# Moving the split weights of a decoder layer's plain products to another place within 256 bytes of SBUF

## The chip, the core and the metric

The kernel runs on one core of a Trainium2 chip. The metric is the device time of one execution in microseconds; lower is better. Most executions of it agree within 0.3%. One further execution was profiled, and all rows shown here come from such profiles.

## What is computed

One layer of a decoder over 512 prompt positions and 64 sample positions (8 sequences of 8), 576 columns together, with D_MODEL = 1024 and D_FF = 2816:

```python
def decoder_layer(x, c, pos0, S0, w_ada, b_ada, ...):
    m = silu(c) @ w_ada + b_ada                  # nine shift/scale/gate vectors
    h = modulate(rms_norm(x, n1_g), sh1, sc1)
    x = x + 0.5 * g1 * swiglu(h, w1_gate, w1_up, w1_down)
    h = modulate(rms_norm(x, nm_g), sh2, sc2)
    mix, S_new, v_rows = token_mix(h, ..., w_in, ..., w_a, w_b, w_o)   # gMLP branch and retention branch, merged
    x = x + g2 * mix
    h = modulate(rms_norm(x, n2_g), sh3, sc3)
    x = x + 0.5 * g3 * swiglu(h, w2_gate, w2_up, w2_down)
    return x, S_new, v_rows

def swiglu(h, w_gate, w_up, w_down):
    return (silu(h @ w_gate) * (h @ w_up)) @ w_down
```

All arrays are float32.

## The kernel before

**Split operands.** The large products run in TensorE's fp32r form. To keep float32 accuracy, every operand is split into a high part (ScalarE casts it, line 187, 195, 669 or 952) and a low part (VectorE subtracts, line 188, 196, 679 or 957). A product of two split operands is three matmuls for each slice of 128 rows of the contraction: high by high, high by low, low by high. Each matmul loads its own 128 x 128 weights first; the weight load of the next matmul runs while the present one streams its moving operand.

**Two kinds of product.** The products with the gate, up and most w_in matrices use a scheme with seven products of half blocks (`prod`, line 651): the moving operand is 288 columns wide. Everything else that multiplies by split weights, the plain products, goes through `proj` (line 485): the down projections w1_down and w2_down (tiles `wd`, some in `whl` and `xw`), w_b, the u columns of w_in and w_a (tiles `whl`) and w_o (tiles `whl`, `xw`, `wd` and one `wo`). `proj` makes an output of 576 columns in two PSUM banks, 320 columns wide and 256 columns wide:

```python
        for k in ks or range(kc):
            xh, xl = X[k]
            for z, (s, m) in enumerate(((wh, xh), (wh, xl), (wl, xh))):
                PE.matmul(
                    ps[:, :PW[h]], lhsT=s[:, k, c0:c0 + P], rhs=m[:, PART[h]],
```

Here `lhsT` is the stationary operand, the weights, and `rhs` the moving one. The values products (lines 1353 and 1583) have the roles the other way round: the operand `xx` is stationary and the split weights `whl` move.

**Places in SBUF.** The tile of a pair of split weights is a few words longer than its content, and `set_in` puts the content some words behind the tile's start:

```python
        t = home.tile([P, n + room], F32R, **kw)[:, at:at + n]
```

`at` is INTO = 28 words (112 bytes) for the seven-product weights and for the weights of lines 1353 and 1583. It is MID for the plain products. What follows counts addresses within one partition, modulo 256 bytes; the rows of all tiles concerned keep that place from slice to slice except where noted. In the compiled program the moving operands of `proj` (tiles `c`, `xx`, `xa`) all begin at 128, and so do the tiles `wd`, `whl` and `xw`; with MID = 16 words their weights lie at 192, which is 64 bytes on from the moving operand. The one tile `wo` (output block 7 of w_o, in the pool `hb_pool`) begins at 0, so its weights lie at 64, which is 192 bytes on. In `prod` the rows of the operand are 1152 bytes, four and a half times 256, so the weights lie 112 and 240 bytes on in turn. In lines 1353 and 1583 the stationary operand lies 144 bytes on from the moving weights.

**Order.** The Tile framework orders instructions by data and by the order in which they are written; at the changes of stage an order written by hand (`BEGIN`, `INTO_MIX`, `INTO_FFN2`) is kept on each engine. Weights come from HBM on the SyncE queue into `wraw` tiles. Three or four tile buffers (`whl`) or two (`wd`) let splits run ahead of the products.

**Names.** `home_wd`, `home1`, `home_whl` and `home_o` choose the tile for one output block's down or w_o weights; `nine_w` is the `xw` home, `whl` the general one. `load_w(..., at=MID)` serves w_b, u and w_a.

Of the kernel before, what the change touches and what calls it, by code (L numbers as in the profile page):

```python
# [35 lines left out]
GROUPS = (5, 6, 5, 6)  # L36

INTO = 28
MID = 16
HALF = (slice(0, H), slice(H, T))  # L40
PART = (slice(0, 320), slice(320, T))
PW = (320, T - 320)
# [42 lines left out]
def layer_kernel(ctx: ExitStack, tc: tile.TileContext, a):  # L85
# [24 lines left out]
    def nm(s):  # L110
        count[0] += 1
        return f"{s}_{count[0]}"
# [5 lines left out]
    def pool(stack, name, side="left"):  # L118
        return stack.enter_context(tc.tile_pool(name=nm(name), bufs=1, side=side, reuse_waits="tile"))
# [17 lines left out]
    def nine_w(shape):  # L137

        room = 9 * 256 - shape[1] * shape[2] * shape[3]
        return set_in(now["xs1"], shape, room, MID, tag="x", name=nm("xw"), bufs=3)  # L140

# [6 lines left out]
    def set_in(home, shape, room=INTO, at=INTO, **kw):  # L148

        n = 1  # L150
        for d in shape[1:]:
            n *= d
        t = home.tile([P, n + room], F32R, **kw)[:, at:at + n]
        if len(shape) == 4:
            return t.rearrange("p (a b c) -> p a b c", b=shape[2], c=shape[3])
        return t.rearrange("p (a b c d) -> p a b c d", b=shape[2], c=shape[3], d=shape[4])
# [9 lines left out]
    def whl(shape, at=INTO):  # L166
        small = len(shape) == 3 and shape[1] == 1
        tag = "whs" if small else "whl"
        return set_in(
            now["whs"] if small else wp, [P] + shape, INTO if small else 64, at,  # L170
            tag=tag, name=nm(tag), bufs=1 if small else 4,
        )
# [18 lines left out]
    def load_w(src, k0, kc, c0, cols, eng=None, at=INTO):  # L191
        return split_w(load_raw(src, k0, kc, c0, cols), eng, at)
# [772 lines left out]
    def home_wd(c, shape):  # L965
        return set_in(now["hl"], shape, 64, MID, tag="wd", name=nm("wd"), bufs=2)

    def home_whl(c, shape):
        return home_wd(c, shape) if c in (0, 1, 4, 5) else whl(shape[1:], MID)

# [163 lines left out]
    def home1(c, shape):  # L1134
        if c in (6, 7):
            return nine_w(shape)
        return home_wd(c, shape) if c in (0, 1, 4, 5) else whl(shape[1:], MID)

# [400 lines left out]
    def weights_b(hds, j):  # L1539
        kc = 2 * len(hds)  # L1540
        return load_w(a["w_b"][0], 2 * hds[0], kc, j * (8 // kc) * P, 8 // kc * P, at=MID)

# [112 lines left out]
    def weights_u(g):  # L1655
        return load_w(win, 0, KC, U0 + g * P, P, at=MID)

# [154 lines left out]
    def home_o(c, shape):  # L1812
        if c < 2:
            return whl(shape[1:], MID)
        if c < 5:
            return nine_w(shape)
        return home_wd(c, shape) if c < 7 else set_in(hb_pool, shape, INTO, MID, tag="wo", name=nm("wo"), bufs=1)

    Wo = Down(a["w_o"][0], 0, KC, home_o)
    late = []  # L1820

# [48 lines left out]
    hb_pool = pool(greg, "hb", "right")  # L1870
# [184 lines left out]
```

## Time and profile before

| | us |
|---|---|
| median of 3 runs (lowest, highest) | 1661.5 (1661.2, 1664.42) |
| the profiled execution | 1662.69 |
| its span, first to last instruction | 1660.9 |
| TensorE matmuls busy (12548 of them) | 1628.6 (98% of the span) |
| VectorE busy | 1153.0 (69%) |
| ScalarE busy | 783.1 (47%) |
| GpSimd busy | 293.4 (18%) |

The mean granted TensorE clock is 0.996. Lines 651 and 485 hold the largest groups of matmuls. A matmul's duration in the rows is longer than the time from its start to the next one's start, because matmuls are pipelined: the duration of "one" holds the way through the array as well as the streaming. Where matmuls run back to back, a stretch of the timeline gives the step from start to start: its length, less one duration, over the count less one.

### The profile page before, as it was taken

To read this page: it belongs to the slowest core of one execution; us is meant where nothing else is said; L and a number is where in the kernel's file an instruction comes from. 1 tells how busy PE (TensorE), PEld (TensorE's weight loads), DVE (VectorE), ACT (ScalarE), POOL (GpSimd) and SP (SyncE) were. 2 spreads that over 40 slices of the span, in tenths; PEclk is the share of its full clock that TensorE was granted. 3 is DMA by queue.
4 is the path that set the end of the run, shared out by engine and by line. 5 is a ranking of instruction groups with operands and counts; after the bars stand their busy time and mean duration, and the time that the engine had idled before them with its cause. 6 is when DMAs were issued, how large, how long until landed. Compare 5 with 4: busy or idle time off the path is not lost. (4 is left out here: it accounts for less than half of the span.)

```text
span 1660.9 us, 31368 instructions
## 1 busy us (share of the span) xinstructions
PE 1628.6 (98%) x12548; PEld 1566.4 (94%) x12548; DVE 1153.0 (69%) x1835; ACT 783.1 (47%) x1331; POOL 293.4 (18%) x372
## 2 busy tenths in 40 slices
PE   7999999999999999999999999999999999999997
PEld 4899999999999999999999999998999999999997
DVE  6867857576697777854788554676748868576773
ACT  5634524344564556553444453453236535343454
POOL 0000000000411111113346343454231000000002
PEclk9999999999999999999999999999999999999999
DMA  9553444332536776765467574799540333332321
GB/s 300 144 157 107 140 135 132 114 104 87 178 118 208 225 217 190 220 192 184 128 195 243 175 176 153 218 257 268 165 140 13 87 93 97 94 90 82 98 88 58
DMA packets 300212, 252.09 MB, mean 152 GB/s; under 512 B 13593, under 2 KB 260633, under 8 KB 300066
## 3 DMA queue, kind: packets, MB, share of 16 engines
q1 hardware_dynamic: 284594, 206.76, 41.3%
q0 software_dynamic: 13168, 40.97, 8.9%
q10 hardware_dynamic: 2304, 2.36, 0.4%
q8 instruction: 98, 1.61, 0.4%
q14 instruction: 48, 0.39, 0.1%
HBM read 207.01 MB, written 43.02 MB: 151 GB/s over the span
## 5 line engine op out<-in xcount | busy, mean ns | idle before, releaser
L651 PE MATMUL ps<-xa,whl 128*128 128x288 f32 x3000 | 422.2, 295 | 6.0 <-ACT xa L564 2.6
L651 PEld LDWEIGHTS ps<-xa,whl 128*128 128x128 f32 x3000 | 403.1, 190 | 18.7 <-issue 5.0
L651 PE MATMUL ps<-xs,whl 128*128 128x288 f32 x2040 | 289.1, 295 | 0.8 <-ACT sn L660 0.6
L651 PEld LDWEIGHTS ps<-xs,whl 128*128 128x128 f32 x2040 | 274.0, 189 | 11.0 <-issue 5.0
L679 DVE TENSOR_TENSOR whl<-wraw,whl 128x1024 fp32r<-128x1024 f32 x192 | 234.3, 1222 | 54.6 <-ACT whl L669 46.4
L669 ACT CAST whl<-wraw 128x1024 fp32r<-128x1024 f32 x192 | 200.0, 1047 | 107.7 <-DVE wraw L793 67.0
L485 PEld LDWEIGHTS ps<-c,wd 128*128 128x128 f32 x1824 | 240.1, 188 | 3.5 <-issue 3.4
L485 PE MATMUL ps<-c,wd 128*128 128x320 f32 (+1 forms) x1824 | 243.3, 294 | 0.0
L485 PE MATMUL ps<-c,whl 128*128 128x256 f32 (+1 forms) x1368 | 189.6, 296 | 1.1 <-ACT c L195 0.7
L485 PEld LDWEIGHTS ps<-c,whl 128*128 128x128 f32 x1368 | 182.0, 188 | 3.3 <-ACT c L195 1.0
L472 POOL TENSOR_TENSOR x<-x,s 128x64 f32<-128x64 f32 x72 | 36.9, 513 | 801.0 <-DVE s L471 773.5
L466 DVE SCALAR_TENSOR_TENSOR x<-ps,gate,x 128x320 f32<-128x320 f32 (+1 forms) x128 | 61.1, 481 | 115.4 <-PE ps L485 115.4
L660 ACT COPY sn<-ps 128x288 f32<-128x288 f32 x195 | 77.2, 398 | 105.1 <-PE ps L651 104.9
L188 DVE TENSOR_TENSOR whl<-wraw,whl 128x1024 fp32r<-128x1024 f32 x56 | 76.6, 1370 | 66.0 <-ACT whl L187 63.4
L952 ACT CAST wd<-wraw 128x640 fp32r<-128x640 f32 (+2 forms) x58 | 45.3, 781 | 105.3 <-PE ps L485 96.0
L1353 PE MATMUL ps<-whl,xx 128*128 128x256 f32 x768 | 88.9, 276 | 0.0
L1353 PEld LDWEIGHTS ps<-whl,xx 128*128 128x128 f32 x768 | 88.1, 188 | 0.0
L651 PE MATMUL ps<-xs,whs 128*128 128x288 f32 x480 | 69.9, 294 | 0.0
L187 ACT CAST whl<-wraw 128x1024 fp32r<-128x1024 f32 x56 | 58.5, 1048 | 22.3 <-PE ps L485 14.2
L651 PEld LDWEIGHTS ps<-xs,whs 128*128 128x128 f32 x480 | 65.7, 189 | 0.0
L669 ACT CAST whs<-wraw 128x512 fp32r<-128x512 f32 x62 | 38.5, 620 | 56.0 <-PE ps L651 46.8
L957 DVE TENSOR_TENSOR wd<-wraw,wd 128x640 fp32r<-128x640 f32 (+2 forms) x58 | 53.3, 920 | 10.6 <-ACT wd L952 10.5
(285 smaller groups left out, 2219.4 us busy)
## 6 DMA issues: line engine op xcount, KB each, us to landing
ada<-in_w_ada_dram SPq DMA_DIRECT2D x56, 512.0 KB
wraw<-in_w_in_dram SPq DMA_DIRECT2D x96, 256.0 KB
wraw<-in_w_gate_dram SPq DMA_DIRECT2D x88, 256.0 KB
wraw<-in_w_up_dram SPq DMA_DIRECT2D x88, 256.0 KB
wraw<-in_w_in_dram SPq DMA_DIRECT2D x32, 512.0 KB
wraw<-in_w_down_dram SPq DMA_DIRECT2D x32, 384.0 KB
wraw<-in_w_down_dram SPq DMA_DIRECT2D x32, 320.0 KB
accd<-c POOLq DMA_DIRECT2D x32, 288.0 KB, 5.4
```

The source lines that it names most:

```text
L187: ACT.copy(out=hi, in_=raw)
L188: now["lo"] = (eng or DVE).tensor_tensor(out=lo, in0=raw, in1=hi.bitcast(F32), op=ALU.subtract)
L466: DVE.scalar_tensor_tensor(out=x[:, o:o + w], in0=ps[:, :w], scalar=g[:, c, 0:1], in1=x[:, o:o + w], op0=ALU.mult, op1=ALU.add)
L472: return lambda: POOL.tensor_tensor(out=x[:, NP:T], in0=x[:, NP:T], in1=u, op=ALU.add)
L485: PE.matmul(ps[:, :PW[h]], lhsT=s[:, k, c0:c0 + P], rhs=m[:, PART[h]], start=k == 0 and z == 0, stop=k == kc - 1 and z == 2,)
L651: PE.matmul(ps[:, :H], lhsT=s[:, j * P:(j + 1) * P], rhs=m[:, j, :], start=fresh and j == 0 and z == 0, stop=j == 3 and z == 2, skip_group ...
L660: ACT.copy(out=t, in_=ps[:, :H])
L669: ACT.copy(out=hl[:, 0], in_=src)
L679: now["lo"] = DVE.tensor_tensor(out=hl[:, 1], in0=src, in1=hl[:, 0].bitcast(F32), op=ALU.subtract)
L952: ACT.copy(out=hl[:, 0], in_=self.raw[c])
L957: DVE.tensor_tensor(out=lo, in0=self.raw[c], in1=hi.bitcast(F32), op=ALU.subtract)
L1353: PE.matmul(ps[:, :DV], lhsT=s, rhs=m, start=i == 0, stop=i == 23)
```

## The change

The constant MID becomes 45 words, and the tile `wo`, which has no room for it, keeps 16. Tile sizes stay as they are. In the places above: the weights of the plain products go from 192 to 52 (308 less 256), that is from 64 to 180 bytes on from the moving operand. `wo` stays 192 on, the seven-product weights and lines 1353 and 1583 stay as they were. All former places are multiples of 16 bytes; 180 is 11 times 16 and 4 more.

```diff
-MID = 16
+MID = 45
...
         if c < 2:
             return whl(shape[1:], MID)
         if c < 5:
             return nine_w(shape)
-        return home_wd(c, shape) if c < 7 else set_in(hb_pool, shape, INTO, MID, tag="wo", name=nm("wo"), bufs=1)
+        return home_wd(c, shape) if c < 7 else set_in(hb_pool, shape, INTO, 16, tag="wo", name=nm("wo"), bufs=1)
```

## The prediction

> **What bounds the kernel now.** I read the page's busy times first, then the chain of waits, then TensorE's own waits, then the groups of instructions by shape, and last single stretches of the timeline.
>
> ```profile
> PE 1628.6 (98%) x12548; PEld 1566.4 (94%) x12548; DVE 1153.0 (69%) x1835; ACT 783.1 (47%) x1331; POOL 293.4 (18%) x372
> ...
> PEclk9999999999999999999999999999999999999999
> ```
>
> TensorE is busy for 98% of the span at full clock. The longest wait of a matmul is 4.4 us, and line 485, the plain products, has two rows in that view, 1.1 us together:
>
> ```profile
> PE ps L302 <- ACT ada L299: 4.4, 1, 4.4
> ...
> PE ps L485 <- ACT c L195: 0.7, 1, 0.7
> ...
> PE ps L485 <- DVE c L196: 0.4, 1, 0.4
> ```
>
> So the time is the number of matmuls by the step from one start to the next, and a change of place in SBUF can matter only through that step. The step isn't one number. Two pieces of the chain of waits hold down products alone, eight output blocks of the second feed-forward part each, half of the matmuls 320 wide and half 256 wide; columns are start, length, line and count:
>
> ```profile
> 1325.37 31.21 PE ps L485 x240
> ...
> 1423.21 38.08 PE ps L485 x288
> ```
>
> 31.21/240 is 130.0 ns for a matmul, 38.08/288 is 132.2 ns, with the same place and the same code. By shape (count, busy us, mean ns of one), the first stage and then the second:
>
> ```profile
> L485 PE MATMUL ps<-c,wd 128*128 128x320 f32 x120 | 18.9, 308 | 0.0
> L485 PE MATMUL ps<-c,wd 128*128 128x256 f32 x120 | 14.9, 276 | 0.0
> ```
> ```profile
> L485 PE MATMUL ps<-c,wd 128*128 128x320 f32 x144 | 22.4, 308 | 0.0
> L485 PE MATMUL ps<-c,wd 128*128 128x256 f32 x143 | 18.1, 281 | 0.0
> ```
>
> The 320-wide matmul is the same in both; the 256-wide one takes 276 ns or 281 ns. It runs in one of two steps, and once in one it stays there for a stage. The 5 ns per 256-wide matmul are half of that per matmul of the mix, which is the 2.2 ns between 130.0 and 132.2.
>
> **The change, part by part.** No instruction, wait, transfer or tile size is added, taken away or moved to another queue. Three sorts of work touch the new place: the weight loads of line 485, the matmuls that stream while the next load reads, and the splits that write there.
>
> *The matmuls.* The trace shows three places at work. At 64 bytes on there are both steps, as above. The nearest rows to 180 lie on either side of it, 192 (tile `wo`) and 144 (line 1353):
>
> ```profile
> 1241.69 3.68 PE L485 MATMUL ps<-xa,wo 128*128 128x320 f32 x24
> ...
> 1253.86 2.88 PE L485 MATMUL ps<-xa,wo 128*128 128x256 f32 x24
> ```
> ```profile
> L485 PEld LDWEIGHTS ps<-xa,wo x48: 187/188/188, 1241.5 to 1256.4; 128*128 128x128 f32 x48
> L485 PE MATMUL ps<-xa,wo x48: 276/292/308, 1241.7 to 1256.5; 128*128 128x320 f32 x24, 128*128 128x256 f32 x24
> ```
> ```profile
> L1353 PE MATMUL ps<-whl,xx x768: 275/275/362, 741.8 to 1101.9; 128*128 128x256 f32 x192
> ```
>
> The first fence is the timeline (start, length, line, count), the others give the shortest, median and longest duration. At 192 the 256-wide step is (2.88 - 0.276)/23 = 113.2 ns, and the 320-wide one (3.68 - 0.308)/23 = 146.6 ns. At 144 the 256-wide matmul takes 275 ns at the median of 768. Both neighbours have the fast 256-wide step, and the one that shows the 320-wide matmul has it as it was. So I take: 256 wide always at 276, 320 wide unchanged at 308.
>
> What that is worth: the groups of the whole run that are 256 wide and move to the new place, with the largest of the 320-wide ones:
>
> ```profile
> L485 PE MATMUL ps<-c,wd 128*128 128x320 f32 x912 | 143.3, 309 | 0.0
> L485 PE MATMUL ps<-c,wd 128*128 128x256 f32 x912 | 115.2, 279 | 0.0
> ...
> L485 PE MATMUL ps<-c,whl 128*128 128x256 f32 x684 | 90.3, 281 | 0.0
> ...
> L485 PE MATMUL ps<-xx,whl 128*128 128x256 f32 x192 | 23.9, 281 | 0.0
> ...
> L485 PE MATMUL ps<-xa,xw 128*128 128x256 f32 x72 | 8.9, 279 | 0.0
> ```
>
> Above 276 these hold 912 x 3 + 684 x 5 + 192 x 5 + 72 x 3 = 7.3 us; the four small groups left over (132 matmuls, `xa,whl`, `xa,wd`, `c,xw`) add at most 0.7 us at 5 ns. That 8.0 us is a ceiling: the means hold matmuls that waited for their data, and those stay (the longest of `c,whl` is 498 ns, in the row below). If the rows were pure mixtures of 276 and 281, 60% of the first and fourth and all of the others would be slow, 1,600 of 1,992; with the waits taken off I put it at half, 1,000, and by 2.2 ns x 2 = 4.4 ns each that is **4.4 us**. The floor of this term is 0 (the slow step stays as frequent), and below nothing it is the 1,000 fast ones turning slow, +4.4 us.
>
> ```profile
> L485 PE MATMUL ps<-c,whl x1368: 276/304/498, 415.9 to 1650.0; 128*128 128x320 f32 x98, 128*128 128x256 f32 x98
> ```
>
> *The 320-wide matmuls.* At 64 and at 192 they take 308 ns. Bounds by one step of the trace, the 5 ns between 276 and 281, either way: 1,992 x 5 ns = 10.0 us less or more. I take 0, the value at the nearest place.
>
> *The weight loads.* A load of 128 columns takes 188 ns; the loads of the `wo` tile never more than that, those of other plain products at times 192 (next fence). They run beside the matmul before, so I cost the change in them at nothing; the matmul of 113 ns is the cover, and what it costs without cover is the rival "one line more" below.
>
> *The splits.* ScalarE's cast of a 1024-column pair takes 1047 ns at place 112 (line 669) and 1048 at place 64 (line 187, MID); VectorE's subtraction 1222 ns (line 679) and 1214 ns in `wo`. So these don't follow the place among multiples of 16 bytes. No row shows a write at another multiple of 4; the slowest group of that shape, line 188, bounds it at 1370 ns, 156 ns more.
>
> ```profile
> L485 PEld LDWEIGHTS ps<-c,wd x1824: 186/188/192, 110.4 to 1643.7; 128*128 128x128 f32 x183
> ```
> ```profile
> L679 DVE TENSOR_TENSOR whl<-wraw,whl 128x1024 fp32r<-128x1024 f32 x192 | 234.3, 1222 | 54.6 <-ACT whl L669 46.4 <-DMA wraw<-in_w_in_dram 1.9 <-DMA ada<-in_w_ada_dram 1.6
> L669 ACT CAST whl<-wraw 128x1024 fp32r<-128x1024 f32 x192 | 200.0, 1047 | 107.7 <-DVE wraw L793 67.0 <-PE ps L651 31.1 <-DMA wraw<-in_w_up_dram 6.3
> ...
> L188 DVE TENSOR_TENSOR whl<-wraw,whl 128x1024 fp32r<-128x1024 f32 x56 | 76.6, 1370 | 66.0 <-ACT whl L187 63.4 <-DMA c<-in_gm_wsT_dram 1.8
> L187 ACT CAST whl<-wraw 128x1024 fp32r<-128x1024 f32 x56 | 58.5, 1048 | 22.3 <-PE ps L485 14.2 <-PE ps L1366 3.8 <-PE ps L1583 2.8
> ```
> ```profile
> L957 DVE TENSOR_TENSOR wo<-wraw,wo x1: 1214/1214/1214, 1225.4 to 1225.4; 128x1024 fp32r<-128x1024 f32 x1
> ```
>
> Some 100 pairs are written there (71 of the down and w_o products, 32 of w_b, u and w_a), so the bound is 16 us of VectorE's time over the whole run. VectorE is idle for 31% of the span and the plain products hardly wait for it, so I take nothing; if it did reach TensorE, the matmuls after a change of stage would show it first, waiting for `wd` or `whl`.
>
> *The sum.* 4.4 us off the profiled execution's 1662.69 gives 1658.3; that execution lies 1.2 us over the median of 1661.5, and its span 1.8 us under its own time. Against the median: 1661.5 - 4.4 = **1657.1 us**.
>
> **The rivals.**
>
> *No change.* Which of the two steps a stage falls into may follow from how the stage before left the pipeline and not from the place. For it: at 64 both appear with the same code. Against it: 768 matmuls at 144 have the fast one at the median. It gives 1661.5. The Trainium skill would have this one, or even less: "TensorE: Matmul & The Clock Gate", Part 2, says that the streaming operand and the weight load have two independent read ports of SBUF, so that loading the next weights takes no read bandwidth from the running matmul. By that rule no place matters and the sum is 0. The next row, of one line and one width, spreads from 289 to 298 ns within a group that hardly waits, and what alternates in it is the place (112 and 240 bytes on), so I give the rule less weight than the neighbours' rows.
>
> ```profile
> L651 PE MATMUL ps<-xs,whs x480: 289/294/298, 68.3 to 1598.7; 128*128 128x288 f32 x160
> ```
>
> *One line more (slower).* 180 is the only place that is no multiple of 16 bytes, so a row of 128 weights (512 bytes) lies in 33 pieces of 16 bytes and not in 32. What a piece costs: a load of 32 columns takes 108 ns and one of 128 takes 188, so 80/96 = 0.83 ns a column and 3.3 ns for four. A whole load of 128 columns reads for about 107 ns by that rate, 6 ns less than the fast step of 113. From the point where the extra piece, or a collision that it causes, is more than these 6 ns, the matmul waits. Paid by each of the 3,984 matmuls, 3.3 ns makes 13.1 us: 1674.6. The same size comes out if the 320-wide matmuls take a step of 5 ns (10.0 us) and the other 256-wide ones fall into the slow step (4.4 us): 1675.9.
>
> ```profile
> L307 PEld LDWEIGHTS ps<-ada,cs x224: 106/108/110, 79.4 to 737.2; 128*32 128x32 f32 x112
> ```
>
> The Trainium skill speaks for this one: "SBUF — State Buffer", section "Door 1: The DMA port swizzle", says that SBUF is read in lines of 16 bytes and that each access that crosses into a new line pays. No run here yet shows a weight load that begins within a line.
>
> *The 320-wide matmul gains a step too (faster).* If the odd place takes the load's reads out of the way of the stream altogether, the 320-wide matmuls fall by 5 ns as well: 1661.5 - 4.4 - 10.0 = 1647.1. For it: a 320-wide step of 146.6 ns is 33.4 ns longer than the fast 256-wide one for 64 columns more, 0.52 ns a column, where the 256-wide one pays 113.2/256 = 0.44, so there is time in it that the columns don't explain: at 0.44 ns it would be 141. Against it: it is 308 ns at both places that the trace has.
>
> **How the numbers follow.** The forecast (256 wide all fast, 320 wide as before) has 0.37. No change has 0.20, the slower rival 0.27 (nothing in the trace rules it out, and it is the only new kind of address), the faster one 0.16. A change of 0.2%, 3.3 us, is about what a measurement of this kernel can tell from none; the forecast's 4.4 us is little over it, so some of it (0.05) counts as no change. Faster: 0.32 + 0.16 = 0.48; same 0.25; slower 0.27. The forecast's own range is 1653.5 (the ceiling of 8.0 us) to 1660. The range to hold 8 in 10 reaches from 1644, a little below the faster rival, to 1675.5, over the slower one's 13.1 us.
>
> **What would show it.** In the changed kernel's rows of line 485 by shape, the 256-wide groups should read 276 to 278 where they read 279 to 281, and the 320-wide ones 308 to 309. The two pieces of the chain that were 31.21 us and 38.08 us should both come to 130.0 ns a matmul. The loads should stay at 188 ns. Lines 651, 1353 and 1583 should not move. The prediction is wrong if the 320-wide rows move at all, if weight loads read over 191 ns (one line more), or if the casts and subtractions into `wd` get longer and TensorE waits for them.

## The result, and the profile after

The changed kernel takes 1656.37 us at the median of six runs (1652.59 to 1658.16), the kernel before 1661.54 us at the median of six beside it (1661.11 to 1664.42). The ratio is 0.9962, with a 95% interval of 0.9948 to 0.9975. The forecast was 1657.1 us. The time came out as forecast; two of the steps that led to it did not.

The page of the changed kernel first. Its span was 1660.9 us before:

```profile
span 1654.4 us, 31368 instructions
...
PE 1624.5 (98%) x12548; PEld 1560.9 (94%) x12548; DVE 1153.0 (70%) x1835; ACT 784.3 (47%) x1331; POOL 293.1 (18%) x372
```

As many matmuls as before, TensorE as full as before, and a span 6.5 us shorter: the matmuls themselves follow each other faster. The chain of waits holds the two stages that the prediction showed, in the same order (start, length, line and count):

```profile
1320.89 30.95 PE ps L485 x240
...
1418.41 36.98 PE ps L485 x288
```

They were 31.21 and 38.08 us. That is now 129.0 ns and 128.4 ns a matmul; the forecast was 130.0 in both. The stage that already ran in the faster step lost time as well, which the forecast has no term for. The groups by shape show where from (count, then busy us and mean ns of one), the whole run first, then the first and the second of the two stages:

```profile
L485 PE MATMUL ps<-c,wd 128*128 128x320 f32 x912 | 140.6, 306 | 0.0
L485 PE MATMUL ps<-c,wd 128*128 128x256 f32 x912 | 114.6, 278 | 0.0
L485 PE MATMUL ps<-c,whl 128*128 128x320 f32 x684 | 111.0, 310 | 1.1 <-ACT c L195 0.7 <-DVE c L196 0.4
L485 PE MATMUL ps<-c,whl 128*128 128x256 f32 x684 | 89.2, 279 | 0.0
L485 PE MATMUL ps<-xx,whl 128*128 128x320 f32 x192 | 29.5, 309 | 0.0
L485 PE MATMUL ps<-xx,whl 128*128 128x256 f32 x192 | 24.0, 281 | 0.0
...
L485 PE MATMUL ps<-xa,wd 128*128 128x256 f32 x48 | 6.0, 285 | 0.0
```
```profile
L485 PE MATMUL ps<-c,wd 128*128 128x320 f32 x120 | 18.5, 306 | 0.0
L485 PE MATMUL ps<-c,wd 128*128 128x256 f32 x120 | 15.1, 277 | 0.0
```
```profile
L485 PE MATMUL ps<-c,wd 128*128 128x320 f32 x144 | 22.0, 306 | 0.0
L485 PE MATMUL ps<-c,wd 128*128 128x256 f32 x144 | 17.6, 276 | 0.0
```

In the first stage the 320-wide matmuls alone gain (18.9 us before); the 256-wide ones, all fast before, are 0.2 us slower. The rows of before that the prediction did not show:

```profile
L485 PE MATMUL ps<-c,whl 128*128 128x320 f32 x684 | 112.5, 312 | 1.1 <-ACT c L195 0.7 <-DVE c L196 0.4
...
L485 PE MATMUL ps<-xx,whl 128*128 128x320 f32 x192 | 30.0, 311 | 0.0
```

The three large groups of 320-wide matmuls went from 143.3 + 112.5 + 30.0 = 285.8 us to 281.1, those of 256-wide ones from 115.2 + 90.3 + 23.9 = 229.4 us to 227.8. With the small groups, line 485 loses 5.4 us in its 320-wide and 1.6 us in its 256-wide matmuls, 7.0 us together. The 6.5 us of the span are these 7.0 less small shifts in other lines and waits.

The rest stayed. These are the loads (shortest, median, longest), and the groups of the lines whose places did not change:

```profile
L485 PEld LDWEIGHTS ps<-c,wd x1824: 186/188/193, 110.3 to 1637.2; 128*128 128x128 f32 x183
```
```profile
L651 PE MATMUL ps<-xs,whl 128*128 128x288 f32 x2040 | 289.1, 295 | 0.9 <-ACT sn L660 0.5
...
L1353 PE MATMUL ps<-whl,xx 128*128 128x256 f32 x768 | 88.9, 276 | 0.0
...
L957 DVE TENSOR_TENSOR wd<-wraw,wd 128x640 fp32r<-128x640 f32 x32 | 27.5, 859 | 5.4 <-ACT wd L952 5.4
L952 ACT CAST wd<-wraw 128x640 fp32r<-128x640 f32 x32 | 23.3, 728 | 63.6 <-PE ps L485 56.1 <-DMA wraw<-in_w_down_dram 4.3 <-DMA wraw<-in_w_gate_dram 3.1
```

The last two, the split of a 640-column pair into `wd`, took 857 ns and 727 ns before.

Below, the *step* is the time from one matmul's start to the next one's, taken from the single records, with steps over 160 ns (waits) left out: some 1,970 steps of 320-wide and 1,983 of 256-wide matmuls. Over the whole run it went from 146.6 to 143.7 ns (320 wide) and from 115.5 to 114.8 ns (256 wide). By that count the change is 1,970 x 2.9 = 5.7 us and 1,983 x 0.7 = 1.4 us, the same picture as the busy times.

### The profile page after: what moved, and what is told of

Same layout as the page of the kernel before. It is cut to its first block, busy times and chain, and to the rows that moved or that the text cites. A ratio compares the mean times of both kernels' runs of the same rounds, so it can differ in the third digit from the quotient of the medians.

```text
span 1654.4 us, 31368 instructions
## 1 busy us (share of the span) xinstructions
PE 1624.5 (98%) x12548; PEld 1560.9 (94%) x12548; DVE 1153.0 (70%) x1835; ACT 784.3 (47%) x1331; POOL 293.1 (18%) x372
## 5 line engine op out<-in xcount | busy, mean ns | idle before, releaser
L651 PE MATMUL ps<-xs,whl 128*128 128x288 f32 x2040 | 289.1, 295 | 0.9 <-ACT sn L660 0.5
L1353 PE MATMUL ps<-whl,xx 128*128 128x256 f32 x768 | 88.9, 276 | 0.0
```

The costliest lines, as they stand in the source:

```text
L651: PE.matmul(ps[:, :H], lhsT=s[:, j * P:(j + 1) * P], rhs=m[:, j, :], start=fresh and j == 0 and z == 0, stop=j == 3 and z == 2, skip_group ...
L1353: PE.matmul(ps[:, :DV], lhsT=s, rhs=m, start=i == 0, stop=i == 23)
```

## The experiments

All edits are against the changed kernel; ratios are to the kernel before, measured beside each.

**Is it the word, the neighbourhood, or the multiple of 4?** After the result there were three readings. One: 180 itself is a good word. Two: any place off a multiple of 16 bytes is, since the reads of load and stream then no longer meet. Three: what decides is the broader neighbourhood, or what the stage before left in the pipeline, so that words near 180 give the same. Four kernels move MID alone; in the first, MID = 44 puts the weights 176 bytes on.

```diff
-MID = 45
+MID = 44
```

> One word less: weights 176 bytes on from the moving operand, on a multiple of 16 bytes. Theory 'place' (only how many bytes on the weights lie decides the step, and the start within a 16-byte line does not): as with 180, 320-wide steps alternate 142 and 145 ns (mean 143.5, duration 306), 256-wide mostly 113.3; about 1656 us, ratio to before 0.996 to 0.998. Rival 'line start' (180 is faster because a row of weights begins off a multiple of 16 bytes, so that the load's reads fall between the stream's): back to 146.7 ns (duration 308) for 320 wide and a mix of 113 and 118 for 256 wide; 1660 to 1662 us, ratio 0.999 to 1.0.

The same line with 17 (68 on, off a multiple of 16 by 4 bytes as 180 is, and on the same place within 16 bytes):

> One word more than before: weights 68 bytes on, off a multiple of 16 bytes by 4 as 180 is. 'Place': as at 64, 320-wide 146.7 ns (duration 308), 256-wide half at 113 and half at 118; 1661 us, ratio 0.999 to 1.001. 'Line start': as at 180, 320-wide 143.5 (306), 256-wide mostly 113; about 1656 us, ratio 0.996 to 0.998.

With 48 (192 on, the place of `wo`, one of the two rows on which the forecast rested):

> Weights 192 bytes on, the place of the tile wo of the kernel before, on which the forecast rested. If that tile's rows stand for the place: 256-wide always 113.3 ns (duration 276), 320-wide 146.6 (308); the gain comes from the 256-wide ones alone, about 4 us, 1657 us, ratio 0.997. If wo only carried on the step that the tiles before it had fallen into ('state'): 256-wide a mix of 113 and 118 as at 64, 320-wide 146.6; 1661 us, ratio 0.999 to 1.001.

With 29 (116 on, 64 bytes ahead of 180, so the same place within 64):

> Weights 116 bytes on: the same place within 64 bytes as 180 (52 past a multiple of 64), one block of 64 bytes earlier, and off a multiple of 16 by 4. If the place within 64 bytes decides: as at 180, 320-wide 143.5 ns (306), about 1656 us, ratio 0.996 to 0.998. If the place within 256 bytes does: nothing ties it to 180; 320-wide then 146.7 or another step (141 to 150), 1650 to 1672 us. 'Line start' alone gives the same as at 180.

All four are slower than the kernel *before*, which no reading of the first three had forecast: ratios 1.0033 (1.002 to 1.0045), 1.0036 (1.0023 to 1.0048), 1.0026 (1.0016 to 1.0035) and 1.0034 (1.0024 to 1.0045). By shape, 176 on and then 192 on:

```profile
L485 PE MATMUL ps<-c,wd 128*128 128x320 f32 x912 | 143.6, 309 | 0.0
L485 PE MATMUL ps<-c,wd 128*128 128x256 f32 x912 | 117.9, 281 | 0.0
```
```profile
L485 PE MATMUL ps<-c,wd 128*128 128x320 f32 x912 | 143.4, 309 | 0.0
L485 PE MATMUL ps<-c,wd 128*128 128x256 f32 x912 | 117.5, 280 | 0.0
```

The 320-wide matmuls are back at 309, and the 256-wide ones are slower than at 64. Four bytes off 180, the gain is gone. So neither the neighbourhood nor the place within 16 or 64 bytes explains it. And the forecast's own support falls: with all plain weights at 192, the place at which the 24 matmuls of `wo` had shown 113.2 ns, the mean step is 117.6 ns.

**The other neighbour, the period, and the weights of the other lines.** MID = 46 is 184 on, the neighbour above. MID = 36 is 144 on, the other row of the forecast (line 1353), now with load and stream in the plain products' roles:

> Weights 184 bytes on, one word past 180. Theory 'window' (good places form a stretch, and 176 lies just outside its lower end): 320-wide steps 143.5 ns or less (duration 306), 256-wide mostly 113; 1653 to 1658 us, ratio 0.995 to 0.998. Theory 'word' (the step is set word by word, and 180 is a single good word): 320-wide 146.7 (308), 256-wide near 118 (281 and over) as at 176 and 192; 1666 to 1670 us, ratio 1.002 to 1.005.

> Weights 144 bytes on, the distance that the values products of line 1353 have with the roles exchanged, and at which all their 256-wide matmuls run at 113.3 ns. If the distance alone sets the step, whichever of the two operands is the weights: 256-wide 113.3 ns (duration 275 to 276); with 320-wide at 146.7 that is 1657 us, ratio 0.997. If the roles matter, or those rows only carry on a fast step: 256-wide near 118 as at 176 and 192, 1666 to 1670 us, ratio 1.002 to 1.005.

184 on gives 1.0027 (1.0017 to 1.0038), 144 on 1.0043 (1.0029 to 1.0057). By shape, 184 and then 144:

```profile
L485 PE MATMUL ps<-c,wd 128*128 128x320 f32 x912 | 143.4, 308 | 0.0
L485 PE MATMUL ps<-c,wd 128*128 128x256 f32 x912 | 117.7, 281 | 0.0
```
```profile
L485 PE MATMUL ps<-c,wd 128*128 128x320 f32 x912 | 143.7, 310 | 0.0
L485 PE MATMUL ps<-c,wd 128*128 128x256 f32 x912 | 119.1, 284 | 0.0
```

180 stands alone between 176 and 184. At 144 the 256-wide matmul takes 284 ns, where line 1353's takes 275, though in both the stationary operand lies 144 bytes on from the moving one. So that row was no neighbour of this case, and distance and width alone don't set the step. What else differs: in line 1353 the weights are the moving operand, its operands begin at other places, and of its three matmuls the first two share the moving operand, where in `proj` they share the stationary one. Which of these counts was not run.

Next the tiles `wd` alone are moved on by 256 bytes more, to ask whether the place counts modulo 256:

```diff
-        return set_in(now["hl"], shape, 64, MID, tag="wd", name=nm("wd"), bufs=2)
+        return set_in(now["hl"], shape, 128, MID + 64, tag="wd", name=nm("wd"), bufs=2)
```

> As the changed kernel, but the weights in the tiles wd (about half of the plain products) begin 64 words further, at 256 + 180 bytes; the others stay at 180. If the place counts modulo 256 bytes: steps of the wd rows as at 180 (320-wide 143.5, 256-wide mostly 113), 1656 us, ratio to before 0.996 to 0.998. If it counts modulo more than 256: wd rows like those at 176 or 192 (146.7 and 118), half of the gain lost and as much added, 1660 to 1664 us.

The ratio is 0.9957 (0.9944 to 0.9969), the same as the change's within the intervals:

```profile
L485 PE MATMUL ps<-c,wd 128*128 128x320 f32 x912 | 140.6, 306 | 0.0
L485 PE MATMUL ps<-c,wd 128*128 128x256 f32 x912 | 114.6, 278 | 0.0
```

So 256 bytes more change nothing that the measurement can tell, where 4 do. Last in this group, INTO = 45 gives the seven-product weights and those of lines 1353 and 1583 the same words behind the tile's start:

```diff
-INTO = 28
+INTO = 45
...
-            now["whs"] if small else wp, [P] + shape, INTO if small else 64, at,
+            now["whs"] if small else wp, [P] + shape, 64, at,
...
-        return home_wd(c, shape) if c < 7 else set_in(hb_pool, shape, INTO, 16, tag="wo", name=nm("wo"), bufs=1)
+        return home_wd(c, shape) if c < 7 else set_in(hb_pool, shape, 28, 16, tag="wo", name=nm("wo"), bufs=1)
```

> As the changed kernel, and the seven-product weights too begin 45 words behind their tile's start: 180 and 52 bytes on in turn (112 and 240 before), the stationary operand of lines 1353 and 1583 76 bytes on from the moving weights (144 before). If 180 is a good word at any width: the 288-wide steps at 180 fall to 127 ns or less; with those at 52 unknown, between 1645 and 1690 us. If a good place is one for a width and a row length: no gain, 131.3 ns stays or rises to 134, 1656 to 1675 us. Lines 1353 and 1583 lose their 113.3 ns for about 118 unless 76 is a good word too: up to 6 us more.

It loses: 1.0046 (1.0033 to 1.0058). Line 485 keeps its gain, and lines 651 and 1353 pay:

```profile
L651 PE MATMUL ps<-xs,whl 128*128 128x288 f32 x2040 | 292.8, 297 | 0.0
...
L485 PE MATMUL ps<-c,wd 128*128 128x320 f32 x912 | 140.6, 306 | 0.0
L485 PE MATMUL ps<-c,wd 128*128 128x256 f32 x912 | 114.6, 278 | 0.0
...
L1353 PE MATMUL ps<-whl,xx 128*128 128x256 f32 x768 | 94.4, 284 | 0.0
```

Line 1353 goes from 276 to 284 ns (88.9 to 94.4 us), the 288-wide matmuls of `xs,whl` from 295 to 297. The words that serve line 485 don't serve these lines.

The seven-product matmuls also show whether the weights' own place counts or their distance from the moving operand; the kernels above move the weights alone and can't tell. The rows of the operand begin at 128 and at 0 in turn, and in the compiled program the tiles `whl` begin at 128, the smaller tiles `whs` at 0. So each distance occurs with two places of the weights. The mean steps between two 288-wide matmuls whose moving operands begin at the same place, from the single records:

| bytes on | kernel | with `whl`, ns | with `whs`, ns |
|---|---|---|---|
| 112 | changed | 129.4 | 129.8 |
| 240 | changed | 132.1 | 132.2 |
| 180 | INTO = 45 | 131.9 | 131.4 |
| 52 | INTO = 45 | 134.6 | 134.3 |

Across a row both operands begin elsewhere and the step stays within 0.5 ns; down a column, from 112 to 240 or from 180 to 52, the weights stay and the step moves by 2 to 3 ns. So the distance counts here. At 180 alone the 288-wide step is 131.4 to 131.9 ns, 2 ns over the one at 112: a word that is good for 320 and 256 columns is not the best for 288.

**Every word at once.** In one kernel each tile of plain-product weights begins at a word of its own, counted on from 0 to 63 as the tiles are made (lines are numbered 8 higher: 485 is 493):

```diff
+WORDS = {"down": 0, "other": 32}
+def word(kind):
+    WORDS[kind] += 1
+    return (WORDS[kind] - 1) % 64
...
-        return set_in(now["hl"], shape, 64, MID, tag="wd", name=nm("wd"), bufs=2)
+        return set_in(now["hl"], shape, 64, word("down"), tag="wd", name=nm("wd"), bufs=2)
...
-        return load_w(a["w_b"][0], 2 * hds[0], kc, j * (8 // kc) * P, 8 // kc * P, at=MID)
+        return load_w(a["w_b"][0], 2 * hds[0], kc, j * (8 // kc) * P, 8 // kc * P, at=word("other"))
...
```

> Every tile of plain-product weights begins at a word of its own: the 64 blocks of the first feed-forward part, of w_o and of the second run through words 0, 1, 2 and so on in the order of their splits, w_b, u and w_a through another round from word 32; wo stays. The step of each place is read from the trace, tile by tile. Theory 'word' (each word has its own step, few are good): 180 shows 143.5 ns (320 wide) and 113 (256 wide) again, 176 and 184 about 146.7 and 118, and at most a handful of the other 60 words come under 145 and 115. Rival 'carry-over' (a tile keeps the step that the tile before it had fallen into): the steps do not follow the word, and 180 in the middle of other words is as slow as they are, 146.7 and 118. The whole: 1662 to 1672 us under either.

One run took 1670.12 us, beside 1664.1 for the kernel before. What counts is inside it: blocks at neighbouring words run one after another in one stage. By shape, the windows of the words 84, 176, 180 and 184, in this order:

```profile
L493 PE MATMUL ps<-c,wd 128*128 128x320 f32 x15 | 2.5, 318 | 0.0
L493 PE MATMUL ps<-c,wd 128*128 128x256 f32 x14 | 2.0, 282 | 0.0
```
```profile
L493 PE MATMUL ps<-c,wd 128*128 128x320 f32 x15 | 2.4, 310 | 0.0
L493 PE MATMUL ps<-c,wd 128*128 128x256 f32 x17 | 2.3, 280 | 0.0
```
```profile
L493 PE MATMUL ps<-c,wd 128*128 128x320 f32 x15 | 2.3, 306 | 0.0
L493 PE MATMUL ps<-c,wd 128*128 128x256 f32 x17 | 2.3, 277 | 0.0
```
```profile
L493 PE MATMUL ps<-c,wd 128*128 128x320 f32 x15 | 2.4, 308 | 0.0
L493 PE MATMUL ps<-c,wd 128*128 128x256 f32 x15 | 2.1, 279 | 0.0
```

(A window of 4 us takes in one or two matmuls of the next tile.) The block at 180 is fast with slow blocks right ahead of it and behind it, so the word makes it fast and it doesn't merely keep the step of the block ahead. The steps of the second half of each tile's matmuls, where they have settled:

| bytes on | 320 wide, ns | 256 wide, ns |
|---|---|---|
| 180 (two tiles) | 143.3, 143.4 | 113.3, 113.4 |
| 12 | 144 | 116.4 |
| 120 | 145.3 | 119.3 |
| 52 | 146.7 | 113.3 |
| 64 (the place before) | 146.9 | 113.2 |
| 76 | 148.7 | 113.3 |
| 88 | 146.3 | 113.3 |
| 176, 184 | 146.7 | 118 |
| 192 | 146.7 | 117.8 |
| 144 | 146.4 | 120 |
| 156 | 151 | 120 |
| 84 | 152.5 | 120.4 |
| 204 (three tiles) | 146.7 to 149.0 | 123.0 to 123.3 |

Most of the 64 words lie at 146.7 and between 117 and 120. 180 has the lowest sum of all. It is the only one that is fast in both shapes: at 52, 64, 76 and 88 the 256-wide matmul is fast and the 320-wide one is not, at 12 nearly the reverse. Most words stand here with one or two tiles, so the table doesn't show how often a place reaches its fast step.

**A word for the seven products.** The same with the weights of line 651 (now 659), everything else as in the changed kernel:

```diff
-            now["whs"] if small else wp, [P] + shape, INTO if small else 64, at,
+            now["whs"] if small else wp, [P] + shape, 64, at,
...
-            hl = whl([2, len(names), 512])
+            hl = whl([2, len(names), 512], word("whl" if len(names) > 1 else "whs"))
```

> The changed kernel with the seven-product weights of each split at a word of its own, words 0 to 63 in turn, four rounds; the plain products stay at 180, lines 1353 and 1583 at 144. Words 28 and 45 are known: 131.2 and 133.4 ns a matmul of 288 columns. Theory 'word': the mean step differs from word to word between some 130 and 137 ns, most near 133, and a word and the word 32 further give about the same, since the two distances of a product change places; if one lies under 131.2 by more than 0.6 ns, it takes over 3.5 us off the whole. Rival: 28 is already the lowest. The whole, with all words mixed: 1660 to 1675 us.

One run took 1662.43 us, beside 1664.26. The large group reads

```profile
L659 PE MATMUL ps<-xs,whl 128*128 128x288 f32 x2040 | 291.9, 296 | 0.3
```

against 289.1 us with all of them at word 28. With the records matched to the program's order, the mean steps of the tiles `whl` lie between 131.3 and 135.0 ns by word. Word 28 takes 132.1 here, and 131.3 in the changed kernel, where every tile has it, so one word's reading is uncertain by nearly 1 ns. Words 60 (131.3), 3 and 35 (both 131.6) read lowest. None is shown to beat 28, and none of these three was run for all tiles.

**A prediction from the sweep.** By the table, 52 on (MID = 13) should be fast for 256 columns and ordinary for 320. If a kernel's time is the sum of its steps, that is worth at most 1,983 x (115.5 - 113.3) ns = 4.4 us, and nothing more:

```diff
-MID = 45
+MID = 13
```

> Weights 52 bytes on, off a multiple of 16 by 4 as 180 is. In the round of all words this place had the step that the forecast gave to 180: 113.3 ns for 256 wide, 146.7 for 320 wide. If the steps of that round add up to the time of the whole, 1,992 matmuls of 256 columns save (115.5 - 113.3) ns and the 320-wide ones nothing: 4.4 us off before, ratio 0.9974, some 1 to 3 us less of it where a row of matmuls needs a few to fall into its step: 0.9974 to 0.999. If one tile's step does not hold for all of them: 256-wide near 118, ratio 1.002 to 1.005.

```profile
L485 PE MATMUL ps<-c,wd 128*128 128x320 f32 x912 | 143.2, 309 | 0.0
L485 PE MATMUL ps<-c,wd 128*128 128x256 f32 x912 | 114.2, 278 | 0.0
```

The ratio is 0.999 (0.9982 to 0.9999): barely faster than before. The 256-wide mean is as good as at 180 or a little better (278 ns, 114.2 us), and the 320-wide one is unchanged. So this kernel has the forecast's mechanism alone, and it is worth about 0.1%, not 0.27%; the rest of the change's gain comes from the 320-wide matmuls.

All the MID kernels together, whole-run steps in ns; "by steps" is 1,970 and 1,983 times the differences to before:

| bytes on | 320 | 256 | by steps, us | measured, us | ratio |
|---|---|---|---|---|---|
| 64 (before) | 146.6 | 115.5 | | | |
| 180 (changed) | 143.7 | 114.8 | -7.1 | -5.2 | 0.9962 |
| 180, `wd` 256 more | 143.7 | 114.8 | -7.1 | -7.6 | 0.9957 |
| 52 | 146.5 | 114.3 | -2.6 | -1.0 | 0.999 |
| 192 | 146.65 | 117.6 | +4.3 | +4.0 | 1.0026 |
| 184 | 146.7 | 117.9 | +5.0 | +5.2 | 1.0027 |
| 116 | 146.7 | 118.7 | +6.5 | +4.7 | 1.0034 |
| 176 | 146.8 | 118.15 | +5.6 | +5.1 | 1.0033 |
| 68 | 146.8 | 118.4 | +6.1 | +4.8 | 1.0036 |
| 144 | 146.9 | 119.0 | +7.5 | +6.6 | 1.0043 |

(Measured: the difference of the medians, with the kernel before measured beside each.) The two columns agree within 2 us with the same sign in all nine: the kernel's time follows the steps. None of the kernels run is faster than the changed one by more than the intervals; the one with `wd` 256 bytes further on equals it.

## Why the prediction was right, and where it was not

**What bounds the kernel** held. TensorE is full, no wait took the place of the steps, and the time follows the step.

**"256 wide always at 276"** was right in kind and mis-sized: 1.6 us by the rows, not 4.4. What failed is "always". In the stage of 288 matmuls the row does read 276. Over the run it reads 278 and 279, 281 in `xx,whl` as before, and 285 in the 48 matmuls of `xa,wd` (281 before). The records of the changed kernel show why. Many rows of matmuls (those of one width that follow each other) begin with some slower steps (118, 119, 122 ns in one) before they settle at 113, 113, 114. Others never settle there: `xa,wd`, which two matmuls of line 444 interrupt, goes 120, 117, 117, 121, 114, 119 and on like that to its end. Taking the second half of each row of 12 or more matmuls, 1,875 matmuls in all without `wo`, 762 stood in rows over 115 ns before and 378 still do. So the prediction's guess that half ran slow was near (41%), but the change makes half of these fast and not all: the mean step comes to 114.8 ns, not 113.3. Nor does a step last for a stage, as the prediction took it: in the kernel before, the eight blocks from 217 us on settle at 113 ns five times and then at 118 three times.

**"320 wide unchanged at 308"** failed: 306, worth 5.4 us. This is the rival "the 320-wide matmul gains a step too", with 2.9 ns in place of 5. What spoke for it in the prediction, that the 320-wide step holds time that its columns do not explain, was right: the settled step alternates between 142 and 145 ns at 180, and at 84 it is 152.5, so 146.7 was no property of the shape. The prediction had named a move of the 320-wide rows as a sign of being wrong, and it came. The two errors, 2.8 us too much in the one term and 5.4 too little in the other, partly cancelled. That the time came out within 1 us of the forecast is luck.

**The neighbours as evidence** failed outright, and this is the step to learn from. 192 and 144 were taken for 180 since they lie on either side of it. The runs at 192 and 144 are 0.26% and 0.43% *slower* than before. A place 4 bytes away tells nothing here. And the 24 matmuls at 192 showed less than they seemed to: in the changed kernel `wo` still lies at 192, and its 256-wide row in the timeline reads

```profile
1248.11 2.99 PE L485 MATMUL ps<-xa,wo 128*128 128x256 f32 x24
```

where it was 2.88 us: (2.99 - 0.281)/23 = 117.8 ns in place of 113.2, with the place and the code unchanged and only the tiles ahead of it moved. In the kernel with the other weights at 52, it is 2.88 us again:

```profile
1253.54 2.88 PE L485 MATMUL ps<-xa,wo 128*128 128x256 f32 x24
```

There, as at 64, one place shows both steps. Had the forecast taken this as "no evidence", its chance for a gain would have been lower, and the MID kernels say that it should have been: of the seven other places run in whole kernels six were slower than before, and the seventh, 52, hardly faster.

**"No change"**, the rival in which the step comes from what ran before and not from the place, is half true for 256 columns: at 64, at 192 and at 180, some rows settle at 113 ns and others near 118. But the place sets how many. Of the same 1,875 matmuls, 258 stand in slow rows at 52, 378 at 180, 762 at 64, 1,791 at 192 and all of them at 68, 116, 144, 176 and 184. For 320 columns it is false: at 180 all but one row of 15 settles below 144.5 ns, at the other places none does. The rule of the Trainium skill that went with it ("TensorE: Matmul & The Clock Gate", Part 2: independent read ports for the streaming operand and the weight load) does not fit these runs: with every instruction the same, the place of the weights alone moves the settled step between 113.3 and 123.3 ns (256 columns, at 180 and 204) and between 143.3 and 152.5 ns (320 columns, at 180 and 84).

**"One line more"** did not happen. The loads read 188 ns at 180 as at 64, and the pieces that the rival priced at 3.3 ns a matmul appear nowhere: 180 is the fastest word and off a multiple of 16, 176 and 192 are multiples and slow. The longest load, 193 ns, is over the 191 that the prediction named as a sign, but it was 192 before; the sign should have been put on the median. Nor do the splits pay: 859 against 857 ns and 728 against 727. The rule of the Trainium skill ("SBUF — State Buffer", "Door 1: The DMA port swizzle": an access that crosses into a new line of 16 bytes pays) shows no cost in these rows, neither for loads nor for the engines' writes.

**Lines 651, 1353 and 1583** were expected to stay. The two shown did, at 295 and 276 ns, and line 1583 read 279 ns before and after.

What stays open is why 180 is good. The runs show that the step depends on the place of the weights, for 288 columns on its distance from the moving operand, to the word, alike after 256 bytes, and differently for 256, 288 and 320 columns and for line 1353. That the reads of load and stream disturb each other, meeting in one of a number of places in SBUF, is the obvious reading, but no run here measures it. Nor is it shown why a row at 64, 180 or 192 falls into one step and not the other.

## What to carry to other kernels

When TensorE is full and the clock is steady, look at the step from start to start by shape and place, not at the mean of a line: identical matmuls with different steps may be time that can be had. The place of the weights against the moving operand, modulo 256 bytes and to the word of 4 bytes, is then worth a sweep, one word a tile in one kernel, because neighbouring words cannot stand for each other and one run shows all of them. Then run the few best words in whole kernels: a row has a slower beginning, and some rows don't reach the fast step at all. Sweep each shape and each kind of product by itself.

## What the runs showed that had not been expected

- The place of the weights sets the settled step of an otherwise equal matmul: 113.2 to 123.3 ns for 256 columns, 143.3 to 152.5 ns for 320. In the 288-wide products it is the distance from the moving operand that counts.
- The effect is one word wide: 180 gives 143.3 and 113.3 ns, 176 and 184 both 146.7 and 118. 256 bytes more change nothing that shows.
- At 180 the 320-wide matmuls do not run at one step but alternate, 142 and 145 ns; the 256-wide ones mostly need a few matmuls to settle at 113, and a fifth of them stand in rows that don't.
- The place of before, 64 on, was itself one of the few good words: of eight other words run in whole kernels, all but 180 and 52 were slower.
- One place can show both 256-wide steps: `wo` at 192 read 113.2 ns in the kernel before and 117.8 in the changed one, with its place and code unchanged.
